# Eight experts on one core: the results kept in SBUF and stored in three transfers behind the last weights

## The chip, the cores and the metric

The kernel runs on one core of a Trainium2 chip. The metric is the device time of one execution in microseconds; a kernel's time is the median of several executions. A core has five engines that run side by side, each with its own list of instructions: TensorE (PE in the profile, its weight loads PEld), VectorE (DVE), ScalarE (ACT), GpSimd (POOL) and SyncE (SP). Transfers between HBM and SBUF run on 16 DMA engines; they are issued by POOL, SP or ACT, and each of the three has a queue of its own.

## The reference

Eight experts each have a batch of 256 rows. Each applies a matrix, a relu and a second matrix.

```python
n_experts, capacity, hidden, expert_hidden = 8, 256, 512, 2048
# x [8, 256, 512], w1 [8, 512, 2048], w2 [8, 2048, 512], all float32
h = np.matmul(x, w1)
h = np.maximum(h, 0)
return np.matmul(h, w2).astype(np.float32)
```

Each expert's w1 and w2 are 4 MB of float32 in HBM, 64 MB for all eight; x and the output are 4 MB each.

## The kernel before, in words

The kernel converts to bf16 as it loads: a transfer issued by POOL reads float32 from HBM and writes bf16 to SBUF, so a weight tile holds 2 MB (the profile counts the bytes written). `load_w1(e)` (L68 to L70) brings one expert's w1 as a tile of 128 partitions by 4 x 2048, `load_w2(e)` (L72 to L76) its w2 as 128 by 16 x 512. Three tiles of each exist at a time, so the load of expert e waits until PE is done with expert e - 3. Most w2 come in one transfer, that of expert 6 in two halves and that of expert 7 in six pieces of 5, 4, 3, 2, 1 and 1 of the 16 rows that a partition holds:

```python
cuts = {E - 2: (0, 8, 16), E - 1: (0, 5, 9, 12, 14, 15, 16)}.get(e, (0, KT2))
```

x is transposed on PE (`transpose_x`, L78 to L95). `first_layer(e)` (L97 to L117) makes 64 matmuls into PSUM at L105, with w1 as the stationary operand, and evicts them with a relu, alternating between ACT (L115) and DVE (L113), into the bf16 tile ht. `second_layer(e)` (L119 to L137) runs over the 16 row blocks kt of w2 and the two halves mt of the batch: 32 matmuls at L125, each 128 x 512, into two PSUM tiles. DVE copies the one (L136) and ACT the other (L137) to the output tile in SBUF. A matmul of block kt needs only the piece of w2 that holds kt.

The order of the work is written out by hand (`manual_schedule`); each engine does its instructions in program order. All weights are loaded through POOL's one queue, in the order 0 to 4 alternating w1 and w2, then w1[5], w1[6], w1[7], w2[5], w2[6], w2[7]. PE does the two layers of experts 0 to 4 in turn, then the first layers of 5, 6 and 7, then their second layers.

The results go out in groups (`STORES`). For a group of two experts there is one output tile from a pool of three; `store` (L139, L140) issues one transfer from POOL. store(0, 1) stands in POOL's list behind the load of w2[4], store(2, 3) behind that of w2[5], ahead of w2[6]; store(4, 5) behind everything that loads, after the second layer of expert 5; store(6) after that of expert 6. The result of expert 7 is stored as two halves, the part that DVE copied from SP (L194) and the part that ACT copied from ACT (L195). POOL's transfers use eight semaphores in turn, so a transfer also waits for the one eight before it; in the kernel before, the last pieces of w2[7] and the stores wait in this way.

Of the kernel before, what the change touches and what calls it, by code (L numbers as in the profile page):

```python
# [9 lines left out]
@with_exitstack  # L10
def kernel(
    ctx: ExitStack,
    tc: tile.TileContext,
    x: bass.AP,
    w1: bass.AP,
    w2: bass.AP,
    out: bass.AP,
):
    nc = tc.nc
    P = 128  # L20
    bf = mybir.dt.bfloat16
    f32 = mybir.dt.float32
    relu = mybir.ActivationFunctionType.Relu

    E, C, H = x.shape
    F = w1.shape[2]
    MT = C // P
    KT1 = H // P
    KT2 = F // P
    WB = 3  # L30


    GROUPS = ((0, 1), (1, 1), (2, 2), (4, 4))

    STORES = ((0, 1), (2, 3), (4, 5), (6,), (7,))


    w1_r = w1.rearrange("e (p kt) n -> e p kt n", p=P)
    w2_r = w2.rearrange("e (p kt) n -> e p kt n", p=P)
    out_r = out.rearrange("e (p mt) n -> p e mt n", p=P)  # L40

    const = ctx.enter_context(tc.tile_pool(name="const", bufs=1))
    wpool = ctx.enter_context(tc.tile_pool(name="weights", bufs=WB))
    hpool = ctx.enter_context(tc.tile_pool(name="hidden", bufs=3))
    opool = ctx.enter_context(tc.tile_pool(name="outs", bufs=3))
    ps_h = ctx.enter_context(tc.tile_pool(name="ps_h", bufs=4, space=bass.MemoryType.PSUM))
    ps_o = ctx.enter_context(tc.tile_pool(name="ps_o", bufs=4, space=bass.MemoryType.PSUM))


    ctx.enter_context(tc.manual_schedule())  # L50

    w1_sb, w2_sb, ht, o_sb = {}, {}, {}, {}
    group_of = {e: g for g, (e0, n) in enumerate(GROUPS) for e in range(e0, e0 + n)}
    x_f = const.tile([P, 4, MT, H], f32, name="x_f")
    x_b = [const.tile([P, n * MT, H], bf, name=f"x_b{g}") for g, (_, n) in enumerate(GROUPS)]
    xt = [const.tile([P, KT1, n, C], bf, name=f"xt{g}") for g, (_, n) in enumerate(GROUPS)]
    identity = const.tile([P, P], bf, name="identity")

    def x_rows(g):
        e0, n = GROUPS[g]  # L60
        return x[e0:e0 + n].rearrange("e c k -> (e c) k").rearrange(
            "(p j) k -> p j k", p=P
        )

    def load_x(g):
        nc.gpsimd.dma_start(x_b[g][:], x_rows(g))  # L66

    def load_w1(e):  # L68
        w1_sb[e] = wpool.tile([P, KT1, F], bf, tag="w1", name="w1_sb")
        nc.gpsimd.dma_start(w1_sb[e][:], w1_r[e])  # L70

    def load_w2(e):  # L72
        w2_sb[e] = wpool.tile([P, KT2, H], bf, tag="w2", name="w2_sb")
        cuts = {E - 2: (0, 8, 16), E - 1: (0, 5, 9, 12, 14, 15, 16)}.get(e, (0, KT2))
        for lo, hi in zip(cuts, cuts[1:]):
            nc.gpsimd.dma_start(w2_sb[e][:, lo:hi, :], w2_r[e, :, lo:hi, :])  # L76

    def transpose_x(g, kts=range(KT1)):  # L78


        n = GROUPS[g][1]
        J = n * MT
        for kt in kts:
            pt = ps_o.tile([P, J, P], bf, tag="ps_o", name="pt_tr")
            for j in range(J):
                nc.tensor.transpose(pt[:, j, :], x_b[g][:, j, kt::KT1], identity[:])  # L86
            src = pt[:].rearrange("p (j m) (e l) -> p m e l j", m=MT, e=n)
            for mt in range(MT):
                dst = xt[g][:, kt, :, mt * P:(mt + 1) * P].rearrange(
                    "p e (l j) -> p e l j", j=J // MT  # L90
                )
                if mt % 2:
                    nc.scalar.copy(dst, src[:, mt])  # L93
                else:
                    nc.vector.tensor_copy(dst, src[:, mt])  # L95

    def first_layer(e, between=()):  # L97
        g = group_of[e]
        xe = xt[g][:, :, e - GROUPS[g][0], :]
        ht[e] = hpool.tile([P, KT2, C], bf, tag="ht", name="ht_sb")  # L100
        for q in range(KT2 // 2):
            ph = ps_h.tile([P, 2, C], f32, tag="ps_h", name="pt_h")
            for i in range(2):
                for kt in range(KT1):
                    nc.tensor.matmul(  # L105
                        ph[:, i, :],
                        w1_sb[e][:, kt, 2 * q + i::KT2],
                        xe[:, kt, :],
                        start=(kt == 0),
                        stop=(kt == KT1 - 1),  # L110
                    )
            if q % 2:
                nc.vector.tensor_relu(ht[e][:, 2 * q:2 * q + 2, :], ph[:])  # L113
            else:
                nc.scalar.activation(ht[e][:, 2 * q:2 * q + 2, :], ph[:], relu)  # L115
            if q % 2 and between:
                between.pop(0)()  # L117

    def second_layer(e):  # L119
        po = [  # L120
            ps_o.tile([P, H], f32, tag="ps_o", name=f"pt_o{mt}") for mt in range(MT)
        ]
        for kt in range(KT2):
            for mt in range(MT):
                nc.tensor.matmul(  # L125
                    po[mt][:],
                    ht[e][:, kt, mt * P:(mt + 1) * P],
                    w2_sb[e][:, kt, :],
                    start=(kt == 0),
                    stop=(kt == KT2 - 1),  # L130
                )
        es = next(es for es in STORES if e in es)
        if e == es[0]:
            o_sb[es] = opool.tile([P, 2, MT, H], f32, tag="o", name="out_sb")
        o = o_sb[es][:, e - es[0]]
        nc.vector.tensor_copy(o[:, 0, :], po[0][:])  # L136
        nc.scalar.copy(o[:, 1, :], po[1][:])  # L137

    def store(*es):  # L139
        nc.gpsimd.dma_start(out_r[:, es[0]:es[-1] + 1], o_sb[es][:, :len(es)])  # L140


    nc.sync.dma_start(x_f[:, :2], x[0:2].rearrange("e (p mt) k -> p e mt k", p=P))
    nc.sync.dma_start(x_f[:, 2:].rearrange("p e mt k -> p (e mt) k"), x_rows(2))
    load_w1(0)
    make_identity(nc, identity)
    load_w2(0)
    load_w1(1)
    load_w2(1)
    load_x(3)  # L150
    load_w1(2)
    load_w2(2)
    nc.scalar.copy(x_b[0][:], x_f[:, 0])  # L153
    nc.scalar.copy(x_b[1][:], x_f[:, 1])  # L154
    for j in (0, 1):
        nc.scalar.copy(x_b[2][:, 2 * j:2 * j + 2, :], x_f[:, 2 + j])  # L156
    transpose_x(0)

    first_layer(0)
    load_w1(3)  # L160
    transpose_x(1)
    second_layer(0)
    load_w2(3)
    first_layer(1)
    load_w1(4)
    transpose_x(2)
    second_layer(1)
    load_w2(4)
    store(0, 1)
    first_layer(2, [lambda kt=kt: transpose_x(3, [kt]) for kt in range(KT1)])  # L170
    load_w1(5)
    second_layer(2)
    first_layer(3)
    load_w1(6)
    second_layer(3)
    first_layer(4)
    load_w1(7)
    load_w2(5)
    store(2, 3)
    load_w2(6)  # L180
    second_layer(4)
    load_w2(7)


    for e in (5, 6, 7):
        first_layer(e)

    second_layer(5)
    store(4, 5)
    second_layer(6)  # L190
    store(6)
    second_layer(7)
    o = o_sb[(7,)]
    nc.sync.dma_start(out_r[:, 7, 0, :], o[:, 0, 0, :])  # L194
    nc.scalar.dma_start(out_r[:, 7, 1, :], o[:, 0, 1, :])  # L195


# [28 lines left out]
```

## Time and profile before

| | |
|---|---|
| median of 9 executions | 183.29 us (183.09 to 183.47) |
| the profiled execution | 183.47 us, its span in the profile 181.3 us |
| PE busy | 126.8 us (70% of the span) |
| ACT, DVE, POOL busy | 33.9 (19%), 32.8 (18%), 15.8 us (9%) |
| bytes | HBM read 71.30 MB, written 4.19 MB: 416 GB/s over the span |
| chain that ended last | DMA 47%, PE 38%, another core or an unknown queue 8% |
| a second-layer matmul at L125 | 379 ns from start to end; 44 in a row took 9.75 us |
| an eviction to the output tile | 0.69 us on DVE, 0.59 us on ACT |
| issue of a weight load on POOL | 0.53 to 0.67 us |

The span is the time between the first and the last event of the profile; the execution's own time has some 2 us around it. Matmuls overlap, so the duration of one is longer than the distance between two. For a transfer the profile gives the time of its issue and the time from the issue to landing; in a deep queue most of the second is waiting, so the useful number is the landing itself, the sum of the two. Where PE waits for a weight tile, the start of its next matmul shows the landing as well. In the slices of the page each digit stands for 4.5 us. In the rows by stretch of time the columns are the length, then the busy time of PE, PEld, DVE, ACT and POOL with the number of instructions, the granted clock, the share of the DMA engines and the GB/s that they wrote; records of DMA engines overlap, so that their share can pass 1.

### The profile page before, as it was taken

How to read it: one execution, taken by the hardware profiler on the slowest of the kernel's cores; microseconds unless marked ns; L12 is line 12 of the kernel's file. 1: busy time of each engine (PE TensorE's matmuls, PEld its weight loads, DVE VectorE, ACT ScalarE, POOL GpSimd, SP SyncE). 2: the span in 40 equal slices, each digit the busy share in tenths (PEclk: the TensorE clock that was granted, in tenths of full speed). 3: DMA queues.
4: the chain of work that ended last, by engine and by line, in shares of the span. 5: the costliest groups of instructions: out<-in, count | busy, mean ns of one | idle time of the engine just before them, and what ended most of it. 6: DMA issues, size and time to landing. Idle time of an engine off the chain costs nothing.

```text
span 181.3 us, 1884 instructions
## 1 busy us (share of the span) xinstructions
PE 126.8 (70%) x825; PEld 89.5 (49%) x832; DVE 32.8 (18%) x56; ACT 33.9 (19%) x61; POOL 15.8 (9%) x33
## 2 busy tenths in 40 slices
PE   0200898979691199969987692926979498997980
PEld 0100695459440189527933691404969386443430
DVE  0100023023401025211311131010324123010110
ACT  2403323023301025111301130011223022010110
POOL 7200001010102000100010006011010101110100
PEclk9999999999999579996999999996999879999996
DMA  5998999999899989998999999999899989999994
GB/s 185 335 260 202 231 221 199 217 231 220 184 231 231 221 184 231 231 217 192 228 231 213 195 228 299 225 217 231 192 228 217 231 192 317 223 214 213 205 355 168
DMA packets 4984, 41.01 MB, mean 226 GB/s; under 512 B 496, under 2 KB 752, under 8 KB 2672
## 3 DMA queue, kind: packets, MB, share of 16 engines
q0 software_dynamic: 4272, 38.27, 95.5%
q1 hardware_dynamic: 560, 2.36, 3.6%
q10 hardware_dynamic: 144, 0.26, 0.4%
q8 instruction: 6, 0.10, 0.2%
q14 instruction: 2, 0.02, 0.0%
HBM read 71.30 MB, written 4.19 MB: 416 GB/s over the span
## 4 chain that ended last, share of the span: by engine, by line
DMA 47%; PE 38%; another core or an unknown queue 8%; POOL 2%; ACT 1%; issue 1%; DVE 1%; POOLq 0%
DMA w_sb<-in_w_dram 47%; PE pt_o L125 19%; PE pt_h L105 18%; PE pt_tr L86 1%; ACT xt L93 1%; POOL w_sb L70 1%; POOL w_sb L76 1%; DVE ht_sb L113 0%; POOL out_dram L140 0%; ACT out_sb L137 0%; DVE xt L95 0%; POOL identity masks.py:199 0%; POOL identity masks.py:197 0%; POOLq masks.py:199 0%
## 5 line engine op out<-in xcount | busy, mean ns | idle before, releaser
L105 PE MATMUL pt_h<-xt,w_sb 128*128 128x256 bf16 x512 | 67.0, 298 | 33.2 <-DMA w_sb<-in_w_dram 22.1
L105 PEld LDWEIGHTS <-w_sb 128*128 128x128 bf16 x512 | 60.7, 148 | 40.2 <-DMA w_sb<-in_w_dram 35.3
L125 PE MATMUL pt_o<-w_sb,ht_sb 128*128 128x512 bf16 x249 | 56.3, 379 | 9.3 <-DMA w_sb<-in_w_dram 6.6
L125 PEld LDWEIGHTS <-ht_sb 128*128 128x128 bf16 x256 | 24.9, 98 | 39.0 <-issue 8.8
L113 DVE TENSOR_SCALAR ht_sb<-pt_h 128x512 bf16<-128x512 f32 x32 | 22.1, 692 | 78.6 <-PE pt_h L105 78.6
L115 ACT ACTIVATE ht_sb<-pt_h 128x512 bf16<-128x512 f32 x32 | 19.1, 598 | 60.5 <-PE pt_h L105 60.5
L137 ACT COPY out_sb<-pt_o 128x512 f32<-128x512 f32 x8 | 4.7, 586 | 60.9 <-PE pt_o L125 60.9
L136 DVE COPY out_sb<-pt_o 128x512 f32<-128x512 f32 x8 | 5.5, 692 | 57.9 <-PE pt_o L125 57.9
L76 POOL DMA_DIRECT2D w_sb<-in_w_dram x14 | 7.6, 540 | 58.4 <-DMA w_sb<-in_w_dram 33.1
L70 POOL DMA_DIRECT2D w_sb<-in_w_dram x8 | 4.5, 558 | 83.0 <-PE pt_h L105 50.8
L86 PE MATMUL pt_tr<-identity,x_b 128*128 128x128 bf16 x64 | 5.1, 230 | 6.8 <-ACT x_b L153 6.8
L86 PEld LDWEIGHTS <-x_b 128*128 128x128 bf16 x64 | 4.6, 117 | 6.8 <-ACT x_b L153 6.8
L95 DVE COPY xt<-pt_tr 128x128 bf16<-128x128 bf16 (+2 forms) x16 | 5.6, 383 | 7.3 <-PE pt_tr L86 7.3
L93 ACT COPY xt<-pt_tr 128x128 bf16<-128x128 bf16 (+2 forms) x16 | 5.2, 377 | 8.0 <-DVE xt L95 8.0
L140 POOL DMA_DIRECT2D out_dram<-out_sb x4 | 2.7, 679 | 13.2 <-ACT out_sb L137 12.9
L156 ACT CAST x_b<-x_f 128x1024 bf16<-128x1024 f32 x2 | 2.0, 1042 | 9.0 <-DMA x_f<-in_x_dram 9.0
L153 ACT CAST x_b<-x_f 128x1024 bf16<-128x1024 f32 x1 | 1.0, 1044 | 3.7 <-DMA x_f<-in_x_dram 3.7
L153 ACT ACT_TABLE_LOAD x1 | 1.3, 1283 | 0.7 <-PEq L210 0.7
L154 ACT CAST x_b<-x_f 128x1024 bf16<-128x1024 f32 x1 | 1.0, 1040 | 0.0
L66 POOL DMA_DIRECT2D x_b<-in_x_dram x1 | 0.6, 558 | 0.0
masks.py:199 POOL TENSOR_SCALAR_AFFINE_SELECT identity<-identity 128x128 bf16<-128x128 bf16 x1 | 0.3, 289 | 0.1
masks.py:197 POOL MEMSET identity<- 128x128 bf16 x1 | 0.2, 224 | 0.0
(4 smaller groups left out, 0.4 us busy)
## 6 DMA issues: line engine op xcount, KB each, us to landing
w_sb<-in_w_dram POOLq DMA_DIRECT2D x14, 2048.0 KB, 47.8
out_dram<-out_sb POOLq DMA_DIRECT2D x3, 1024.0 KB, 45.8
x_f<-in_x_dram SPq DMA_DIRECT2D x2, 1024.0 KB, 10.2
w_sb<-in_w_dram POOLq DMA_DIRECT2D x2, 1024.0 KB, 51.6
x_b<-in_x_dram POOLq DMA_DIRECT2D x1, 1024.0 KB, 48.8
w_sb<-in_w_dram POOLq DMA_DIRECT2D x1, 640.0 KB, 49.1
w_sb<-in_w_dram POOLq DMA_DIRECT2D x1, 512.0 KB, 46.5
out_dram<-out_sb POOLq DMA_DIRECT2D x1, 512.0 KB, 9.0
```

The lines of the kernel that those rows point to most:

```text
L70: nc.gpsimd.dma_start(w1_sb[e][:], w1_r[e])
L76: nc.gpsimd.dma_start(w2_sb[e][:, lo:hi, :], w2_r[e, :, lo:hi, :])
L86: nc.tensor.transpose(pt[:, j, :], x_b[g][:, j, kt::KT1], identity[:])
L93: nc.scalar.copy(dst, src[:, mt])
L95: nc.vector.tensor_copy(dst, src[:, mt])
L105: nc.tensor.matmul(ph[:, i, :], w1_sb[e][:, kt, 2 * q + i::KT2], xe[:, kt, :], start=(kt == 0), stop=(kt == KT1 - 1),)
L113: nc.vector.tensor_relu(ht[e][:, 2 * q:2 * q + 2, :], ph[:])
L115: nc.scalar.activation(ht[e][:, 2 * q:2 * q + 2, :], ph[:], relu)
L125: nc.tensor.matmul(po[mt][:], ht[e][:, kt, mt * P:(mt + 1) * P], w2_sb[e][:, kt, :], start=(kt == 0), stop=(kt == KT2 - 1),)
L136: nc.vector.tensor_copy(o[:, 0, :], po[0][:])
L137: nc.scalar.copy(o[:, 1, :], po[1][:])
L140: nc.gpsimd.dma_start(out_r[:, es[0]:es[-1] + 1], o_sb[es][:, :len(es)])
```

## The change

All eight results get one tile in SBUF, `o_sb`, 32 KB in each partition, in place of the three tiles of 8 KB. Nothing is stored between the weights. store(0, 5), 2.5 MB, is issued by POOL behind the load of w2[7], with the results of experts 0 to 4. store(5, 7), 1 MB, is issued after the second layer of expert 6, and store(7, 8), 0.5 MB, after that of expert 7. All three go through POOL's queue; SP and ACT store nothing. w2[6] is loaded whole, w2[7] in two halves. The order of the instructions on PE, DVE and ACT stays the same, but for ACT's store; in the kernel before, the output copies of experts 6 and 7 also waited for a DMA semaphore (that of an earlier store from the same buffer), and now each waits for PE alone.

```diff
-    STORES = ((0, 1), (2, 3), (4, 5), (6,), (7,))
...
-    opool = ctx.enter_context(tc.tile_pool(name="outs", bufs=3))
...
+    o_sb = const.tile([P, E, MT, H], f32, name="out_sb")
...
-        cuts = {E - 2: (0, 8, 16), E - 1: (0, 5, 9, 12, 14, 15, 16)}.get(e, (0, KT2))
+        cuts = (0, KT2 // 2, KT2) if e == E - 1 else (0, KT2)
...
-        es = next(es for es in STORES if e in es)
-        if e == es[0]:
-            o_sb[es] = opool.tile([P, 2, MT, H], f32, tag="o", name="out_sb")
-        o = o_sb[es][:, e - es[0]]
-        nc.vector.tensor_copy(o[:, 0, :], po[0][:])
-        nc.scalar.copy(o[:, 1, :], po[1][:])
-
-    def store(*es):
-        nc.gpsimd.dma_start(out_r[:, es[0]:es[-1] + 1], o_sb[es][:, :len(es)])
+        nc.vector.tensor_copy(o_sb[:, e, 0, :], po[0][:])
+        nc.scalar.copy(o_sb[:, e, 1, :], po[1][:])
+
+    def store(e0, e1):
+        nc.gpsimd.dma_start(out_r[:, e0:e1], o_sb[:, e0:e1])
...
     load_w2(4)
-    store(0, 1)
     first_layer(2, [lambda kt=kt: transpose_x(3, [kt]) for kt in range(KT1)])
...
     load_w2(5)
-    store(2, 3)
     load_w2(6)
     second_layer(4)
     load_w2(7)
...
     for e in (5, 6, 7):
         first_layer(e)

+    store(0, 5)
     second_layer(5)
-    store(4, 5)
     second_layer(6)
-    store(6)
+    store(5, 7)
     second_layer(7)
-    o = o_sb[(7,)]
-    nc.sync.dma_start(out_r[:, 7, 0, :], o[:, 0, 0, :])
-    nc.scalar.dma_start(out_r[:, 7, 1, :], o[:, 0, 1, :])
+    store(7, 8)
```

## The prediction

> **What bounds the kernel now.** I read the page's slices first, then its queues, then the engines' rows in order of time. The page:
>
> ```profile
> DMA  5998999999899989998999999999899989999994
> ...
> q0 software_dynamic: 4272, 38.27, 95.5%
> ```
>
> After the first slice the DMA engines are full until the last slice, and nearly all of it is POOL's one queue. PE is busy for 70% of the span, so it cannot be what the whole kernel waits for. TensorE's rows in order of time say where it does wait:
>
> ```profile
> 143.55 8.88 PE L105 MATMUL pt_h<-xt,w_sb 128*128 128x256 bf16 x64 [2.42 <-DMA w_sb<-in_w_dram]
> 153.23 7.07 PE L125 MATMUL pt_o<-w_sb,ht_sb 128*128 128x512 bf16 x31 [0.81 <-DMA w_sb<-in_w_dram]
> 160.63 3.61 PE L125 MATMUL pt_o<-w_sb,ht_sb 128*128 128x512 bf16 x16 [0.33 <-DMA w_sb<-in_w_dram]
> 165.46 10.60 PE L125 MATMUL pt_o<-w_sb,ht_sb 128*128 128x512 bf16 x47 [1.22 <-DMA w_sb<-in_w_dram]
> ```
>
> Each row starts when a weight tile has landed, so the starts are a clock of the queue: w1[7] 143.55, w2[5] 153.23, first half of w2[6] 160.63, second half 165.46. The gap before 143.55 reaches back to w1[6] at 133.92, so one whole weight of 2 MB takes about 9.65 us (9.63, 9.68), and a half 4.83. The step from 153.23 to 160.63 is 7.40, one half and something of 2.57 before it: that is store(2, 3), which stands ahead of w2[6] in the same queue. So a 1 MB store costs the queue about 2.57 us even in the middle of the weight stream; it is not hidden beside the loads. store(0, 1) was issued at 56.22 and took the longest landing, 58.3 us, so it came in at 114.5, 2.5 us after w2[4] (PE restarts at 112.01).
>
> Behind the last weights it goes on without a break. The rows of POOL, SP and ACT with the landing times:
>
> ```profile
> 156.03 0.53 POOL L76 DMA_DIRECT2D w_sb<-in_w_dram  x1 [2.03 <-DMA out_dram<-out_sb]
> 161.40 0.71 POOL L140 DMA_DIRECT2D out_dram<-out_sb  x1 [4.83 <-ACT out_sb L137]
> 170.16 0.57 POOL L140 DMA_DIRECT2D out_dram<-out_sb  x1 [8.04 <-ACT out_sb L137]
> ```
> ```profile
> 176.60 0.34 SPq L194 DMA_DIRECT2D out_dram<-out_sb  x1
> 176.71 0.38 ACTq L195 DMA_DIRECT2D out_dram<-out_sb  x1
> ```
> ```profile
> out_dram<-out_sb POOLq DMA_DIRECT2D x1, 512.0 KB, 9.0
> ...
> out_dram<-out_sb SPq DMA_DIRECT2D x1, 256.0 KB, 3.4
> out_dram<-out_sb ACTq DMA_DIRECT2D x1, 256.0 KB, 3.7
> ```
> ```profile
> DMA to landing us min/median/max: 19.4/45.5/67.1
> ```
>
> The last row is that of the weight loads at L76: the shortest landing, 19.4, belongs to the last piece (issued 156.03), so w2[7] is complete at 175.43. The six stores' landings have a median of 12.8, between 9.0 and the next, so store(4, 5) took 16.6 us: 161.40 + 16.6 = 178.0. store(6) lands at 170.16 + 9.0 = 179.16, SP's half of the last result at 180.0, ACT's at 180.41. From 175.43 on that is 1 MB in 2.57, 0.5 MB in 1.16, 0.5 MB in 1.25. The end of the kernel is the DMA engines running dry, not PE's last copy at 176.68 and a latency after it. The span ends at 181.3, 0.89 later, and the execution took 183.47, 2.17 more. That execution is the slowest of nine with a median of 183.29, so I work out a difference and take it from the median.
>
> **The change part by part.** It removes no byte. All eight results, 4 MB, and all 16 weights still cross the same 16 engines.
>
> *Stores moved.* store(0, 1) and store(2, 3) leave the weight stream: 2.5 + 2.57 = 5.07 us, so everything from w2[6] on lands 5.07 earlier (w1[5] to w2[5] 2.5 earlier). Behind the weights there are now 4 MB where there were 2. At the rate of the two POOL stores there (1.5 MB in 3.73 us, 2.49 per MB) that is 9.95, against 4.98 now: 4.97 more. Net gain 0.10.
>
> *Six pieces become two.* w2[7] took 175.43 - 165.46 = 9.97 in six pieces; a whole weight 9.65 to 9.68. The two halves of w2[6], 9.67 together, show that cutting in two costs nothing. Gain 0.29. Weights then end at 175.43 - 5.07 - 0.29 = 170.07, and the stores at 180.02: **0.39 earlier** than 180.41.
>
> *PE.* w2[6] now counts when it is whole, at 165.46 - 5.07 = 160.39, about when its first half came before, so the missing cut costs nothing. 44 matmuls in a row took 9.75, so 32 take 7.09: layer 6 ends at 167.5, layer 7 at 174.6 (its halves land at 165.2 and 170.1, both ahead of it). PE finishes 1.5 earlier, and it isn't late at the end. Evictions stay 0.69 and 0.59. The new copies wait for PE alone.
>
> *POOL.* w2[7]'s first half waits for layer 4's second matmuls, as before (119.37); the second half and store(0, 5) follow at once. With 128 rows the store's issue took 0.57, with 256 0.71; 640 rows would be 1.2, with nothing urgent behind it. Its copies were done at 120. The pieces' waits for DMA, 33.1 us, go; they gated only the queue's far end, 20 us ahead of need. Loads remain queued deep enough: the last wait for layers, w1[7] at 108.86, still comes before w2[4] lands at 112.
>
> *The last store goes through POOL*, in one piece, instead of through SP and ACT. It waits for the last copies: 174.6 + 0.61 = 175.2. The time from a POOL issue to its first bytes on an idle queue isn't in the trace. From below, SP's and ACT's stores, issued at 176.6: the DMA share dips and is back within about 0.9 us.
>
> ```profile
> 176.50:177.50 1.00, 0.00 (x0) 0.00 (x0) 0.07 (x1) 0.18 (x1) 0.00 (x0) 1.00 0.64 260
> 177.50:179.00 1.50, 0.00 (x0) 0.00 (x0) 0.00 (x0) 0.00 (x0) 0.00 (x0) 0.74 0.93 358
> ```
>
> From above, the kernel's first weight: issued at 1.25, it landed 16.6 us later at 17.85; its own 9.65 and the 2.5 of the second x load beside it leave 4.4. I take 1.1 (0.9, plus POOL's issue of 0.57 for SP's 0.34), the row of the same size and direction. First bytes are then possible at 176.3. store(5, 7) keeps the last engine until 170.07 + 3.5 x 2.49 = 178.8. So 2.5 us cover it, and the price is nothing; at 4.4 it would be 179.6, 0.8 late. A loss and a gain both stay in the range.
>
> A rule speaks against this edit. The Trainium skill, "DMA: Bandwidth & Descriptors", section "Issuing engine by pattern", gives plain stores to Sync, and its section "Specifications" puts the first byte at about 1 us for POOL's path and 0.6 for the others. No run here shows 1 us for POOL; by the page the estimate is 0.4 later than by SP, inside the cover of 2.5, and the sum is the same.
>
> *PE's clock* is the other thing that can eat that cover. The rows of each microsecond (busy time of PE, PEld, DVE, ACT and POOL, then granted clock, DMA share, GB/s) after the 2.42 us wait shown above:
>
> ```profile
> 143.00:144.00 1.00, 0.45 (x4) 0.46 (x5) 0.00 (x0) 0.00 (x0) 0.21 (x1) 1.00 1.15 246
> 144.00:145.00 1.00, 1.00 (x7) 0.83 (x6) 0.00 (x0) 0.00 (x0) 0.32 (x1) 0.54 1.23 262
> 145.00:146.00 1.00, 1.00 (x7) 0.77 (x6) 0.00 (x0) 0.60 (x1) 0.00 (x0) 0.50 0.69 147
> ```
>
> The clock was halved for some 3.4 us (144.1 to 147.5). Layer 5 would now end at about 150.7 + 7.1 = 157.8 and layer 6 wait 2.6 us, a new wait of the same length. A half-clock stretch costs 3.4 / 2 = 1.7: PE ends at 176.3, first bytes at 178.0, still 0.8 ahead of 178.8. So nothing again, but the cover is thin. The Trainium skill, "TensorE: Matmul & The Clock Gate", section "Why this matters for your kernels", asks only that idle gaps stay under some 3 us; by it a 2.6 us wait costs nothing and PE ends at 174.6. The 2.42 us row disagrees, and I go by the row.
>
> **Sum.** 0.10 + 0.29 = 0.39 us: 183.29 - 0.39 = **182.9**, own range 182.5 to 183.3.
>
> **Rivals.**
> *The stores in the stream cost more than I charged.* w2[4] took 112.01 - 101.36 = 10.65, 1.0 more than its peers, just ahead of store(0, 1). If the store did that, the stream gains 1.0 more: 181.9. Against it: the load ahead of store(2, 3) took 9.68. 18 in 100.
> *The last weights bound, and stores run free beside PE.* Then the end follows PE, 1.5 us earlier: 181.8. Against it: 2.57 us per store wherever it stands. 5 in 100.
> *Nothing moves.* The pieces' 0.29 is regained elsewhere, or the longer run of stores is a little slower per MB: 183.3. 15 in 100.
> *Slower: the last store starts late.* One mechanism: the 0.5 MB behind PE's end reaches the engines after they ran dry. It decides when layer 7's end + 0.61 + POOL's latency passes 178.8: a latency of 3.6 at full clock, of 1.9 after one half-clock stretch. With the stretch and 3.2 (the middle of 1.9 and 4.4): 176.3 + 0.61 + 3.2 + 1.25 = 181.36, 0.95 after 180.41, so 184.2; with 4.4, 185.4. For it: the 2.6 us wait is new, and in the kernel before two more queues shared the start. Against it: the nearest row says 0.9. 20 in 100.
>
> **Chances.** Forecast 42, rivals 18, 5, 15, 20. About 0.2%, 0.37 us, is what a measurement of this kernel can tell from no change; 182.9 lies at that edge, so I split the forecast 23 to 19, the larger part to faster because the dip to 0.64 in the DMA share can only be filled. Faster 23 + 18 + 5 = 46; same 19 + 15 = 34; slower 20. The range of 181.8 to 184.2 takes in all fast cases but their far ends and about half of the slow one.
>
> **What would show it.** Right: no store among the weights; PE starting layer 6 near 160.4; store(0, 5) landing near 176.3, store(5, 7) near 178.8, the last near 180.0; a DMA share near 1 to 179. Wrong: a last row of a store landing more than 1.3 us after the one before it, with a hole in the DMA share ahead of it (slow rival); w2[4] in 9.65 (first rival); stores far from 2.49 us per MB; a w2[7] of 9.97 in two pieces.

## The result and the profile after

The changed kernel takes 182.45 us (182.34 to 182.70, 9 executions), the kernel before in the same rounds 183.27 (29 executions): a ratio of 0.9957, with a 95% interval of 0.9949 to 0.9965. That is 0.82 us faster, where 0.39 was forecast: outside the forecast's own 182.5 to 183.3 by 0.05, inside the wide range of 181.8 to 184.2. The profiled execution took 182.53 with a span of 180.7; that of before 183.47 with 181.3.

The DMA engines are as full as they were. The page of the changed kernel:

```profile
DMA  6999998999899899989998999999899989999993
...
q0 software_dynamic: 3664, 38.80, 95.7%
```

TensorE's rows show the landings of the weights, here w2[4], w1[5], w2[5] and w2[6]:

```profile
110.94 7.07 PE L123 MATMUL pt_o<-w_sb,ht_sb 128*128 128x512 bf16 x31 [1.05 <-DMA w_sb<-in_w_dram]
120.62 8.88 PE L103 MATMUL pt_h<-xt,w_sb 128*128 128x256 bf16 x64 [2.61 <-DMA w_sb<-in_w_dram]
...
150.12 7.07 PE L123 MATMUL pt_o<-w_sb,ht_sb 128*128 128x512 bf16 x31 [2.85 <-DMA w_sb<-in_w_dram]
159.41 13.97 PE L123 MATMUL pt_o<-w_sb,ht_sb 128*128 128x512 bf16 x63 [2.22 <-DMA w_sb<-in_w_dram]
```

w2[6] is complete at 159.41 where it was at 165.46, 6.05 earlier, 1.0 more than the two stores explain. The microsecond stands at w2[4]: PE waits for w1[4] until 101.26 in this kernel (101.36 before) and for w2[4] until 110.94 (112.01), so that load took 9.68 in place of 10.65. From 159.41 PE runs both last layers without a stop and ends at 173.4.

The three stores, first their issues on POOL, then their landing times on the page:

```profile
119.35 0.89 POOL L134 DMA_DIRECT2D out_dram<-out_sb  x1
167.57 0.75 POOL L134 DMA_DIRECT2D out_dram<-out_sb  x1 [47.33 <-ACT out_sb L131]
174.46 0.56 POOL L134 DMA_DIRECT2D out_dram<-out_sb  x1 [6.14 <-ACT out_sb L131]
```
```profile
out_dram<-out_sb POOLq DMA_DIRECT2D x1, 2560.0 KB, 56.0
...
out_dram<-out_sb POOLq DMA_DIRECT2D x1, 1024.0 KB, 10.3
out_dram<-out_sb POOLq DMA_DIRECT2D x1, 512.0 KB, 4.6
```

They land at 175.35, 177.87 and 179.06: 2.5 us for the 1 MB, 1.2 for the last 0.5 MB. In the rows by stretch the DMA share has no dip any more; it stays at 1 up to 177.5 and then only runs down:

```profile
175.00:176.50 1.50, 0.00 (x0) 0.00 (x0) 0.00 (x0) 0.00 (x0) 0.03 (x1) 0.82 1.02 421
176.50:177.50 1.00, 0.00 (x0) 0.00 (x0) 0.00 (x0) 0.00 (x0) 0.00 (x0) 0.50 1.01 414
177.50:179.00 1.50, 0.00 (x0) 0.00 (x0) 0.00 (x0) 0.00 (x0) 0.00 (x0) 0.50 0.32 128
```

The last landing is 1.35 earlier than before (180.41 to 179.06), yet the span is only 0.6 shorter: it now ends 1.6 after the last landing, and ended 0.9 after it. The end can be read on the line that closes the program (L211 here, L221 before). There each engine has instructions of the kind DRAIN, and the engines then wait for one another through semaphores. A row gives the number of instructions, their shortest, median and longest duration in ns, and the first and last start. First the kernel before, then the changed one:

```profile
L221 POOLq DRAIN  x3: 51/88/10172, 170.1 to 181.0; - x3
```
```profile
L211 POOLq DRAIN  x3: 45/95/5571, 174.4 to 180.5; - x3
```

POOL's long drain starts with its last store and ends at 170.1 + 10.17 = 180.3 in the kernel before, and at 174.4 + 5.57 = 180.0 in the changed one, 1.1 and 0.9 us after the landing of POOL's own last store (179.16 and 179.06). Before, ACT's later landing at 180.41 hid this; now nothing does.

### The profile page after: what moved, and what is told of

The parts are those of the page before. It is cut to its first block, busy times and chain, and to the rows that moved or that the text cites. A ratio compares the mean times of both kernels' runs of the same rounds, so it can differ in the third digit from the quotient of the medians.

```text
span 180.7 us, 1870 instructions
## 1 busy us (share of the span) xinstructions
PE 125.6 (69%) x825; PEld 89.1 (49%) x832; DVE 32.9 (18%) x56; ACT 33.9 (19%) x61; POOL 12.6 (7%) x27
## 4 chain that ended last, share of the span: by engine, by line
DMA 46%; PE 35%; another core or an unknown queue 8%; issue 4%; POOL 1%; ACT 1%; DVE 1%; POOLq 0%
DMA w_sb<-in_w_dram 46%; PE pt_h L103 18%; PE pt_o L123 16%; PE pt_tr L84 1%; ACT xt L91 1%; POOL w_sb L68 1%; POOL w_sb L74 0%; DVE ht_sb L111 0%; POOLq L211 0%; DVE xt L93 0%; POOL identity masks.py:199 0%; POOL identity masks.py:197 0%; POOLq masks.py:199 0%; POOLq L200 0%
## 5 line engine op out<-in xcount | busy, mean ns | idle before, releaser
L103 PE MATMUL pt_h<-xt,w_sb 128*128 128x256 bf16 x512 | 65.8, 294 | 29.5 <-DMA w_sb<-in_w_dram 17.6
L103 PEld LDWEIGHTS <-w_sb 128*128 128x128 bf16 x512 | 59.8, 147 | 36.0 <-DMA w_sb<-in_w_dram 30.9
L68 POOL DMA_DIRECT2D w_sb<-in_w_dram x8 | 4.4, 554 | 85.4 <-PE pt_h L103 53.3
L74 POOL DMA_DIRECT2D w_sb<-in_w_dram x9 | 4.9, 545 | 23.3 <-PE pt_o L123 15.5
L134 POOL DMA_DIRECT2D out_dram<-out_sb x3 | 2.2, 735 | 53.5 <-ACT out_sb L131 53.5
## 6 DMA issues: line engine op xcount, KB each, us to landing
x_f<-in_x_dram SPq DMA_DIRECT2D x2, 1024.0 KB, 10.8
```

The lines of the kernel that those rows point to most:

```text
L103: nc.tensor.matmul(ph[:, i, :], w1_sb[e][:, kt, 2 * q + i::KT2], xe[:, kt, :], start=(kt == 0), stop=(kt == KT1 - 1),)
```

## The experiments

My theory, after the result: the bytes keep their price wherever they stand; the gain beyond the forecast is a microsecond that the first store cost the stream; and part of it is lost again at the end because the last store is POOL's. The main rivals: the microsecond is a mishap of one profile, the end is the same for every queue, or the pieces explain the rest. Comparisons by ratio are with the kernel before in the same rounds.

**The kernel before, once more.** No edit.

> The kernel before, unchanged, profiled once more. In the first profile w2[4] took 10.65 us instead of 9.68, just ahead of store(0, 1), and in the changed kernel 9.68. Theory A (the lost microsecond belongs to the first store of the run, wherever it stands): 10.6 again, span 181.1 to 181.4. Rival B (a mishap of that one execution): 9.7 and a span of about 180.4. Both: the last landing is followed by about 0.9 us to the span's end.

Measured: 183.27 in its one execution, span 181.1. PE waits for w1[4] until 101.20 and for w2[4] until 111.79, 10.59 us. Rival B falls. The two kernels with a changed tail or changed pieces below, which keep store(0, 1) in its place, show 10.57 and 10.72.

**The pieces alone.**

```diff
-        cuts = {E - 2: (0, 8, 16), E - 1: (0, 5, 9, 12, 14, 15, 16)}.get(e, (0, KT2))
+        cuts = (0, KT2 // 2, KT2) if e == E - 1 else (0, KT2)
```

> The kernel before with w2[6] whole and w2[7] in two halves, nothing else. Theory (the small pieces cost the queue 0.23 to 0.29 us and nothing else hangs on them): 183.0, ratio 0.9985, w2[7] in about 9.7 us. Rival (the pieces keep PE from ending late, so that without them layer 7 ends after its last landing plus more than before): same or slower, 183.3 to 184, with a hole in the DMA share ahead of the last store.

Measured: 186.81, ratio 1.0202 (1.0180 to 1.0224). The theory's number was wrong by 3.8 us, and the rival's mechanism is what happened, with a larger price than I gave it. The last row of PE in this kernel, and the rows by stretch and the store behind it:

```profile
165.23 15.66 PE L125 MATMUL pt_o<-w_sb,ht_sb 128*128 128x512 bf16 x64 [5.02 <-DMA w_sb<-in_w_dram]
```
```profile
178.00:180.00 2.00, 2.00 (x11) 0.89 (x10) 0.00 (x0) 0.00 (x0) 0.00 (x0) 1.00 0.01 4
180.00:181.00 1.00, 0.89 (x5) 0.19 (x2) 0.29 (x1) 0.07 (x1) 0.00 (x0) 1.00 0.00 0
181.00:182.00 1.00, 0.00 (x0) 0.00 (x0) 0.40 (x1) 0.51 (x1) 0.00 (x0) 1.00 0.00 0
182.00:183.00 1.00, 0.00 (x0) 0.00 (x0) 0.00 (x0) 0.00 (x0) 0.00 (x0) 1.00 0.72 272
```

With w2[6] whole, PE starts layer 6 at 165.23 in place of 160.63 and has 64 matmuls ahead of it: it ends at 180.9, 4.8 later than before. Some 1.7 us of this are a slower clock: the wait ahead of 165.23 is 5.02 us, the granted clock is 0.50 from 166 to 168, and the 64 matmuls take 15.66 us where 64 take 13.97 in the two kernels below with the last store from SP and ACT, or from SP. The DMA share is near 0 from 178 to 182: all bytes but the last are stored, and the DMA engines wait for PE. The pieces are worth 3.5 us while the stores stand ahead of w2[6], and nothing once they are gone.

**The first four results alone.** Two transfers of 1 MB behind the last weights, from one tile for all results as in the changed kernel (store(0, 2) is its form for experts 0 and 1); pieces and the rest of the tail as before.

```diff
-    store(0, 1)
...
-    store(2, 3)
...
+    store(0, 2)
+    store(2, 4)
     second_layer(5)
```

> The kernel before with its stores of experts 0 to 3 (two transfers of 1 MB) behind the last weights, from one tile for all results; pieces and tail as before. Theory (bytes keep their price of 2.5 us per MB wherever they stand; what is gained is the microsecond at w2[4]): 0.1 from the move and 0.9 from w2[4], minus whatever the first store costs at its new place: last landing 179.4 to 180.3, time 182.3 to 183.1. Rival (the microsecond is a mishap of one profile): 183.2, no difference.

Measured: 183.31, ratio 0.9994 (0.9979 to 1.0009): no difference. But the rival's reason isn't it. w2[4] took 9.64 (101.28 to 110.92), and the last landing came at 179.45, as the theory said. The end ate the gain: SP's and ACT's halves now landed first (179.0 and 179.2), POOL's store of expert 6 last, and the span ended 1.9 after it. The drain row of this kernel:

```profile
L214 POOLq DRAIN  x3: 51/88/15064, 165.5 to 181.1; - x3
```

165.5 + 15.06 = 180.6, 1.15 after the landing.

**The changed kernel with the last store from SP and ACT.**

```diff
-    store(7, 8)
+    nc.sync.dma_start(out_r[:, 7, 0, :], o_sb[:, 7, 0, :])
+    nc.scalar.dma_start(out_r[:, 7, 1, :], o_sb[:, 7, 1, :])
```

> The changed kernel with its last store (expert 7) in two halves from SP and ACT as before, in place of POOL's. In the changed kernel the span ends 1.6 us after the last landing, before 0.9. Theory (the 0.75 is the price of a last store through POOL: SP reaches the wait for it early in its list, and POOL joins the final barrier 0.5 late): last landing 179.1 again, span 180.0, time 181.7 to 181.9, ratio 0.992. Rival (the end has a fixed cost that the profile only places differently, or the two halves lose in the transfer what the barrier gains): 182.3 to 182.6.

Measured: 181.78, ratio 0.9916 (0.9903 to 0.9929). The last landing stays at 179.2 and the span ends at 180.1. As the theory said: 0.7 us of the changed kernel is the end of POOL.

**The same with one store from SP.**

```diff
-    store(7, 8)
+    nc.sync.dma_start(out_r[:, 7:8], o_sb[:, 7:8])
```

> The changed kernel with its last store whole through SP in place of POOL. Theory (what counts is that the last landing isn't POOL's): as with two halves, 181.7 to 181.9; the single wait for both copies costs 0.1 at an issue that is covered by the queue. Rival (both queues of SP and ACT are needed to catch up): over 182.1.

Measured: 181.62, ratio 0.9915 (0.9898 to 0.9931), span 179.9. With the version before, whose interval overlaps, this is the fastest complete kernel of the study. Its drain row, SP's issue and the landing time:

```profile
L211 POOLq DRAIN  x3: 45/102/11161, 167.4 to 179.6; - x3
```
```profile
173.93 0.35 SPq L185 DMA_DIRECT2D out_dram<-out_sb  x1
```
```profile
out_dram<-out_sb SPq DMA_DIRECT2D x1, 512.0 KB, 5.1
```

POOL is done at 167.4 + 11.16 = 178.6, ahead of SP's landing at 173.93 + 5.1 = 179.03, and costs nothing.

**The kernel before with its last store through POOL.**

```diff
-    nc.sync.dma_start(out_r[:, 7, 0, :], o[:, 0, 0, :])
-    nc.scalar.dma_start(out_r[:, 7, 1, :], o[:, 0, 1, :])
+    store(7)
```

> The kernel before with its last store (expert 7) whole through POOL, nothing else. Theory (POOL joins the final barrier 0.9 to 1.15 us after its own last landing, which SP's and ACT's later landings hid until now): last landing 180.4, end 1.6 to 1.9 after it in place of 0.9, time 184.0 to 184.4, ratio 1.004 to 1.006. Rival (the end is the same for each queue, and one transfer of 4 KB rows beats two of 2 KB): 183.2.

Measured: 184.01, ratio 1.0036 (1.0024 to 1.0048). The last landing is at 180.48, as in the kernel before, and the drain ends at 177.2 + 4.47 = 181.7:

```profile
L219 POOLq DRAIN  x3: 51/87/4472, 177.2 to 182.1; - x3
```

So the price of a last store through POOL appears when it is added and goes when it is taken away, at unchanged landings. The 0.77 us here hide a part of it. The span grew by 1.1 (the medians are 182.2 and 181.1), while the time around it fell from 2.17 to 1.79 in the profiled executions, for a reason that the last experiment and the next section take up. POOL issues 28 transfers here, 21 in the changed kernel, and its drain ends 1.19 after its last landing in place of 0.90; that fits the higher price.

**The changed kernel with the pieces of before.**

```diff
-        cuts = (0, KT2 // 2, KT2) if e == E - 1 else (0, KT2)
+        cuts = {E - 2: (0, 8, 16), E - 1: (0, 5, 9, 12, 14, 15, 16)}.get(e, (0, KT2))
```

> The changed kernel with w2[6] in two and w2[7] in six pieces again. Theory (the stores ahead of w2[6] were what made PE need the pieces; with the stores gone PE ends 5 us before the queue does, and the pieces cost only their 0.25 us of transfer): last landing 179.3 to 179.4, layer 7 still ended by 174, time 182.6 to 182.8. Rival (pieces help in this kernel as well, as they do in the kernel before, where their absence cost 3.4): 182.3 or less, with layer 7 ending earlier than 173.4 and the end following it.

Measured: 182.81, ratio 0.9976 (0.9967 to 0.9985), 0.36 above the changed kernel. Here the pieces let PE run the last three layers in a row from 150.06, 20.88 us, to 170.9; that is 2.5 earlier than without them, and it buys nothing. Most of the 0.36 isn't the transfer of the pieces, as the theory had it: the last landing is at 179.1 as in the changed kernel, and not at 179.3 to 179.4. POOL's drain ends 1.11 us after it in place of 0.90, with 26 transfers from POOL in place of 21.

**store(0, 1) moved one load back.**

```diff
     load_w2(4)
-    store(0, 1)
...
     load_w1(5)
+    store(0, 1)
```

> The kernel before with store(0, 1) one load later, behind w1[5] instead of w2[4]. Theory A (the loss goes with the store): w2[4] 9.7, w1[5] 10.5 to 10.7, all else as before, 183.3. Rival B (it belongs to w2[4]'s time, 105 to 112 us): w2[4] 10.6, w1[5] 9.7. Rival C (the store's descriptors must lie long in the queue): smaller than 1 us at either.

Measured: 183.46 in one execution. PE's rows for w2[4], w1[5] and w1[6]:

```profile
110.84 7.07 PE L125 MATMUL pt_o<-w_sb,ht_sb 128*128 128x512 bf16 x31 [1.09 <-DMA w_sb<-in_w_dram]
121.69 8.56 PE L105 MATMUL pt_h<-xt,w_sb 128*128 128x256 bf16 x64 [3.78 <-DMA w_sb<-in_w_dram]
133.87 8.88 PE L105 MATMUL pt_h<-xt,w_sb 128*128 128x256 bf16 x64 [3.62 <-DMA w_sb<-in_w_dram]
```

w2[4] takes 9.66 (from 101.18), w1[5] 10.85. The loss goes with the store; rival B falls. Rival C forecast a smaller loss, which didn't come, but the store still lay some 50 us in the queue (73.86 to 124.1), so it is tested better by the second store of the kernel before: that one lay 46 us (109.91 to 155.8) and cost its bytes alone.

**store(0, 1) alone moved behind the weights,** so that store(2, 3) is the first; again from one tile for all results.

> The kernel before with the store of experts 0 and 1 alone moved behind the last weights; that of 2 and 3 stays ahead of w2[6] and is now the first store of the run. Theory A (the first store with loads queued behind it costs a microsecond at the load ahead of it): w2[4] 9.7, w2[5] 10.5 to 10.7. Rival B (it belongs to the place of store(0, 1), not to being first): w2[4] and w2[5] both 9.6 to 9.8. Both: the end follows POOL's last landing by 1.6 to 1.9 if POOL's store lands last.

Measured: 183.72 in one execution. w2[4] took 9.68; w2[5] 10.83 (139.91 to 150.74). The store and the half weight behind it were shorter by 0.3 and 0.1 than before, so some 0.7 of it is a real loss. In the kernel before, the load ahead of the same store(2, 3), then the second, took 9.68. Theory A holds, with a smaller size.

**An earlier first store, through SP.** Expert 0 is stored from SP after its second layer, expert 1 from POOL at the old place.

```diff
     load_w2(3)
+    nc.sync.dma_start(out_r[:, 0], o_sb[(0, 1)][:, 0])
...
-    store(0, 1)
+    nc.gpsimd.dma_start(out_r[:, 1], o_sb[(0, 1)][:, 1])
```

> The kernel before with the store of experts 0 and 1 split: expert 0 from SP right after its second layer (about 40 us), expert 1 from POOL at the old place. The first store of the run costs a microsecond at the load ahead of it (w2[4] 10.6; w1[5] 10.8 and w2[5] 10.8 when the first store was moved there). If it is the first write of the run on any queue: a loss near 40 us and w2[4] 9.7. If it is the first store in POOL's own queue behind loads: w2[4] 10.5 to 10.7 again. Either way the end stays within 0.5 of the kernel before, 182.9 to 183.8.

Measured: 182.88 in one execution. w2[4] took 9.68 (102.77 to 112.45), so being the first store in POOL's own queue isn't enough for the loss. But it didn't appear near 40 us either: w1[3] landed at 83.39, and in the kernels with nothing stored up to there mostly at 81.7 to 82.0; 0.5 MB alone is 1.25. So a first store through SP costs 0.2 to 0.4 more than its bytes. POOL's first store is also half as large here as elsewhere (0.5 MB in place of 1), and no run separates its size from the earlier store through SP.

**The disputed latency by itself.** The changed kernel without store(0, 5) and store(5, 7), so the results of experts 0 to 6 are left out of the output.

```diff
-    store(0, 5)
...
-    store(5, 7)
```

> The changed kernel without the stores of experts 0 to 6, which are left out of the output: only store(7, 8) remains, through POOL, when the queue is empty. Measures the disputed time from a POOL issue to its landing on an idle queue. Prediction's value (first bytes 1.1 us after issue, 1.25 for 0.5 MB, some 0.4 for receipt): 2.7 to 3.0 us from issue to landing. Its upper bound (4.4 to first bytes): 6 us. End after the landing by 1.6 (POOL's own end follows its last landing by about 0.9), so a span of 178.6 to 179.2, or 182 with the upper bound.

Measured: 180.60 in one execution, span 178.8. The issue of the only store, its landing time and the rows by stretch:

```profile
174.35 0.54 POOL L134 DMA_DIRECT2D out_dram<-out_sb  x1 [55.09 <-ACT out_sb L131]
```
```profile
out_dram<-out_sb POOLq DMA_DIRECT2D x1, 512.0 KB, 2.9
```
```profile
175.00:175.25 0.25, 0.00 (x0) 0.00 (x0) 0.00 (x0) 0.00 (x0) 0.00 (x0) 1.00 0.00 0
175.25:175.50 0.25, 0.00 (x0) 0.00 (x0) 0.00 (x0) 0.00 (x0) 0.00 (x0) 1.00 0.28 115
175.50:175.75 0.25, 0.00 (x0) 0.00 (x0) 0.00 (x0) 0.00 (x0) 0.00 (x0) 1.00 0.93 377
```

The DMA engines are idle until 175.25 and busy from about 175.4: 1.1 us after the issue. The whole store takes 2.9 us.

**More transfers for the same bytes.** From the version with the last store through SP.

```diff
-        cuts = (0, KT2 // 2, KT2) if e == E - 1 else (0, KT2)
+        cuts = (0, KT2 // 2, KT2) if 3 <= e else (0, KT2)
...
-    store(0, 5)
+    for e in range(5):
+        store(e, e + 1)
...
-    store(5, 7)
+    store(5, 6)
+    store(6, 7)
```

> The kernel with the last store through SP, with more transfers of the same bytes: w2[3] to w2[7] each in two halves, and each expert's result stored by itself, 32 transfers in all and none from ACT. The time around the span (execution minus span) was 2.06 to 2.20 us in the six kernels with 31 or 32 transfers and 1.77 to 1.79 in the seven with 20 to 30. Theory (it depends on the number of transfers): 2.1 to 2.2 around a span of 179.9 to 180.3, 182.0 to 182.5. Rival (it hangs on something else that those six share, such as stores from POOL, SP and ACT beside six pieces): 1.77 to 1.79 around the same span, 181.6 to 182.1.

Measured: 182.48 in one execution, span 180.4, so 2.07 around it. The theory's direction holds, just below its range of 2.1 to 2.2; the span is 0.1 longer than expected. Here POOL issues 29 transfers, and its drain ends at 179.65, after SP's landing at 179.27, so POOL's end shows although the last store is SP's.

## Why the prediction was right, and where its sum was not

It was right in sign and range, and its main reason held: the same bytes cross the same engines, and the last landing comes when these run dry. Its two terms, forecast at 0.39, came to some 0.3 of the 0.82. The rest is three terms that it had put at nothing: a gain of 1.0, a loss of 0.7 and a gain of 0.4. That they partly cancel, and that the time so came near the forecast, is luck. By its own list of signs the first rival came true (w2[4] in 9.65; it took 9.68), and that rival's 181.9 missed the time by about as much as the forecast did (0.55 and 0.45). Step by step:

*Stores moved, 0.10.* Right. store(0, 5), store(5, 7) and store(7, 8) need 10.0 us from the last weight (169.1) to 179.06, 2.49 per MB as forecast.

*Six pieces to two, 0.29.* Right within 0.1 in the changed kernel: w2[7] takes 9.7 to 9.8 in place of 9.97. Putting the pieces back costs 0.36, but 0.2 of this is POOL's longer drain, a price of the number of transfers that the prediction didn't have. The reason given for the missing cut, that w2[6] comes whole when its half came before, holds only because of the other half of the change. Alone the edit costs 3.5 us, a part of it through the clock. The prediction named the condition and not its price, and that was the largest number in the whole change.

*The stores in the stream.* This is the term that was mis-sized. I charged store(0, 1) its 2.5 us and left the extra microsecond of w2[4] to a rival with 18 in 100, on the ground that the load ahead of store(2, 3) took 9.68. That comparison was unfair: store(2, 3) was the second store. Five profiles with a first store in POOL's queue among the weights show 0.9 to 1.2 us more at the load ahead of it, wherever that is, and a sixth a net 0.7; in those without such a store w2[4] takes 9.6 to 9.7. The gain is 0.97.

*The end.* The span was taken to end 0.89 after the last landing, as before. That step failed: the 0.89 belongs to a kernel whose last landing isn't POOL's. It became 1.6, a loss of 0.7, shown by the last store moved to SP (181.62) and, in the kernel before, to POOL (184.01, with 1.9 after the last landing).

*Around the span.* 183.47 - 181.3 = 2.17 became 182.53 - 180.7 = 1.8. I took it as constant. In the fourteen profiles it is 2.06 to 2.20 with 31 or 32 transfers and 1.77 to 1.79 with 30 or fewer. All other executions agree, with their spans known to 0.1: 1.73 to 1.85 with up to 30, 2.02 to 2.24 with 31 or 32. It is a step and not a price of each transfer: the kernel before with its last store through POOL has 30 in place of 31 and lies at 1.75 to 1.85 in all nine of its executions, with all its pieces. The last experiment went from 1.77 to 2.07 with more transfers, without small pieces and without a store from ACT. So some 0.4 of the gain goes with the transfers saved (31 to 23). That no other cause is behind it rests on the one execution of the last experiment, and what the time is spent on isn't in the profile.

The sum as it was in the two profiles: 0.1 + 0.2 + 1.0 - 0.7 + 0.4 = 1.0, against 0.94 measured between these two executions, and 0.82 between the medians.

*The slow rival.* Its mechanism, a last store that comes after the engines ran dry, didn't happen. The latency was 1.1, the value taken, and not 1.9 to 4.4. POOL's issue came 1.08 after PE's end (173.38 to 174.46), not the 0.61 assumed; the cover of 2.5 us took that easily. The kernel before already had it: POOL's issue at 161.40 came 0.47 after the end of ACT's copy (160.34 + 0.59). As for the clock, I went by the row in which a wait of 2.42 us was followed by a half clock. Here layer 6 waited 2.22 us and the clock stayed whole:

```profile
159.00:160.00 1.00, 0.59 (x3) 0.29 (x3) 0.00 (x0) 0.00 (x0) 0.00 (x0) 1.00 0.82 172
160.00:161.00 1.00, 1.00 (x7) 0.47 (x5) 0.00 (x0) 0.00 (x0) 0.00 (x0) 1.00 1.25 262
```

The Trainium skill, "TensorE: Matmul & The Clock Gate", section "Why this matters for your kernels", would have it so, since the gap is under its 3 us. But in the kernel with the last store from SP and ACT the wait of 2.52 us ahead of w1[7] was followed by 64 matmuls in 8.87 us, where the usual is 7.21. The changed kernel itself has both, in its rows above: after 2.61 us ahead of w1[5] 64 matmuls took 8.88 us, at a granted clock of 0.50 from 122 to 124, and after 2.85 us ahead of w2[5] the clock stayed at 1.00. So the length of the wait alone doesn't decide, neither by the rule nor by my row. The Trainium skill, "DMA: Bandwidth & Descriptors", section "Issuing engine by pattern", which gives plain stores to Sync, was right for this kernel's last store by 0.8 us (182.45 to 181.62). The first byte isn't what decided: the last landing stayed at 179.0 to 179.1. The same page's section "Specifications" has about 1 us to the first byte for POOL's path, and the run with one store shows 1.1.

*Open.* Why a first store costs the load ahead of it a microsecond, why the loss is absent after an earlier first store through SP (or with a first store of half the size), and what the time around the span does at more than 30 transfers. In all fourteen profiles the load of w1[1], near 28 to 38 us, also took 10.4 to 10.8, before the first byte of any store; whether that microsecond has the same cause isn't known.

## What to carry to other kernels

In a kernel bound by its transfers, list the landings: here a transfer that was only moved kept its price, but for the load ahead of the first store. Then look at what the order changes at its ends, which queue lands last and what the closing barrier waits for. Two edits that look independent must be priced alone and together: the pieces were worth 3.5 us with the stores ahead of them and cost 0.36 without. A forecast that comes out near the time can still have missed several terms that cancel, so compare term by term. A step that is longer than its peers deserves a test before it is called a mishap, and so does the time around the span.

## What the runs showed of the hardware

POOL's last drain ended 0.8 to 1.2 us after the landing of POOL's own last transfer in every profile, whatever the other queues did. The delay goes with the number of transfers that POOL issued in the whole kernel, at 0.04 us for each: 0.82 with 19, 0.86 with 20, 0.90 with 21, 0.94 with 22, 1.11 with 26, 1.15 with 27, 1.19 with 28, 1.23 with 29. A last store through POOL cost 0.7 to 0.8 us more than one through SP or through SP and ACT where POOL issued 21 transfers, and 1.1 us of span where it issued 28. On an idle queue POOL's store of 0.5 MB has its first bytes 1.1 us after the issue and lands after 2.9. The first store of a run, standing in POOL's queue among loads, made the load ahead of it 0.7 to 1.2 us longer, but not in the run with an earlier store through SP; behind the last load it cost nothing that shows. The time outside the span differed by 0.3 to 0.4 us between kernels with 30 transfers or fewer and with 31 or 32. After waits of 2.2 to 2.9 us TensorE's clock was halved in some places and whole in others (2.61 us and 2.85 us in the changed kernel).
